# Hybrid attention and RWKV-7 decoder step: RWKV inputs through DRAM, one evicting engine per scan half-step, a rotating bank for odd scans, other queues for stores

## The chip, the cores and the metric

One core of a Trainium2 chip runs the whole program. The time is device microseconds of one execution, lower is better. The kernel before takes 2656.18 us, the median of three runs (2654.99, 2656.18, 2662.91).

The engines are named as the profile names them: PE (TensorE, matrix products; PEld is its weight load), DVE (VectorE), ACT (ScalarE), POOL (GpSimd), SP (the engine that here only issues DMAs). A "q" behind a name (SPq, ACTq, POOLq) means that engine's DMA issues.

## What is computed

One decoder layer, 2048 wide, for a prompt of 512 tokens and 8 single-token decode requests that share the weights. Everything is f32. The part around the change is the first sub-layer:

```python
h = _modulate(_rmsnorm(x, g_norm_mix[l]), sh1, sc1)        # adaLN: sh1 .. gt2 = silu(c) @ w_ada + b_ada
proj = h @ w_in[l]
q, k, v, p_rwkv = jnp.split(proj, ATTN_SPLITS, axis=-1)
...                                                        # sliding-window attention on q, k, v
rw, S, last_row = _rwkv7_mix(p_rwkv, shift0, S0, ...)
x = x + gt1[:, None, :] * (jnp.concatenate([att, rw], axis=-1) @ w_out[l])
...                                                        # then a SwiGLU feed-forward, then a final norm
```

RWKV-7 has 16 heads of 64. From the columns of `p_rwkv` (each mixed with the row of the token before) come r, k, v, a decay w, a gate, and vectors a and b. Per token and head a 64 x 64 state moves on:

```python
sa = jnp.einsum("bhij,bhj->bhi", S, a_t)
S = S * w_t[:, :, None, :] + sa[..., None] * b_t[:, :, None, :] + v_t[..., None] * k_t[:, :, None, :]
y = jnp.einsum("bhij,bhj->bhi", S, r_t)
```

The outputs are the two y, the new keys and values, the new RWKV states and the shift rows.

## The kernel before

**Main products.** Each f32 weight tile is split into a high part `wh` (a cast on ACT) and a low part `wl` (a subtraction on DVE), and the activations into H and L; a product is three fp32r matmuls, wh x H, wh x L and wl x H (`unit`, `mm3`, L98). `main_tile` makes one 128-column tile of `proj`: 16 k steps, each of 6 matmuls (128x128 weights, 260 columns: 256 tokens and 4 decode rows per half), with a new 128x512 weight tile every 4 k steps. `w_in` has 39 such column tiles: 5 are made in the startup (three tiles of low-rank inputs, and the first k and r tiles), 34 in the RWKV stage: 22 further RWKV inputs (k, r and v of 8 head pairs, less the two made early) and 12 for attention, which are "spilled" to DRAM (`filler`, tiles `sp`).

**Background work.** The RWKV work and the rest of the adaLN product run as Python generators beside the main tiles. After every k step `pump` adds 0.62 us to a reckoned PE clock and lets each generator whose own reckoned time has come emit its next piece. So the code writes its instructions in an interleaved order. A scheduler then orders them: each engine takes the earliest written instruction that its model holds ready, so the final order can differ from the written one where something is not ready yet.

**The RWKV chain of a head pair** (8 pairs, hp = 0 .. 7):
- `w_in_tile(8+hp)`, `(hp)`, `(16+hp)` make k, r and v. Each is evicted by ACT into a tile `pc`, of which there are four (the "ring"); a tile is held in PSUM, or spill tiles are put in ahead, until a ring place is free.
- `rwkv_prep1`: token shift (`shift_mix`, on POOL and DVE), the low-rank decay and rate products (PE tiles `pw`, `pa`, with weights `lf`), exponentials, norms and reciprocals, then transposes and small products per 32-token chunk (`pT`, `pG`). The chunk matrix `AB` goes to DRAM (`ABd`) and comes back spread over partitions (`As`) by four DMAs.
- `rwkv_prep2`: the same for r and v (`pA`, `pb`; tiles `RR`, `LS`, `BV`).
- `rwkv_rest`: a triangular solve of 31 steps on DVE (`stmp`, `Tt`), again a round trip through DRAM (`TTd`, `Td`), products `pu`, and then **the scan**: 16 chunks, each of two half-steps. Half-step A multiplies `L3` (128 rows by 32 columns, two heads) with the state tile `Z` into one PSUM tile `psc` and evicts 32x64 per head to Z: head 0 by DVE, head 1 by ACT. Half-step B multiplies `LS` (128 by 64) with Z into `psc` and evicts 64x64 per head, scaled by the chunk's decay `PC`: head 0 by DVE, head 1 by ACT. Each half-step needs the one before. Then come `pY`, a group norm, the gate (`pg`) and a store to `catd`.

Small products stand on PE between main products. The adaLN generator (`ada_gen`) adds one group of 4 matmuls (128x32 weights, tile `ada`, input tile `ar`) per k step; the `ar` tiles (three of them) also take what is spilled.

**Queues.** SP issues all weight loads, half of the `As` and `TTd` transfers, the spills and the stores to `catd`. POOL issues the other half.

**Behind the stage** come attention, the output projection (`po`), and the feed-forward (more than half of the time), none of which the diff edits.

Of the kernel before, what the change touches and what calls it, by code (L numbers as in the profile page):

```python
# [7 lines left out]
F32 = mybir.dt.float32  # L8
# [6 lines left out]
P = 128  # L15
# [13 lines left out]
I_WA, I_G0, I_G1 = 24, 25, 26  # L29

# [21 lines left out]

class PacedCore:
# [10 lines left out]
class Kern:  # L64
    def __init__(self, tc, I, O, upto="all"):
        self.tc, self.nc, self.I, self.O, self.upto = tc, tc.nc, I, O, upto
# [67 lines left out]
    def start(self, gen):  # L134
        self.bg.append([gen, 0.0])
# [13 lines left out]
    def run(self):  # L149
        tc, nc, I = self.tc, self.nc, self.I  # L150
        R = dict(side="right")
        with ExitStack() as st:
# [3 lines left out]
            self.load_consts()  # L156
            self.catd = [self.dr.tile([P, 512], F32, name=f"catd{i}") for i in range(16)]
# [10 lines left out]
            with ExitStack() as st2:  # L168
# [28 lines left out]
                self.drain()  # L197
                right.close()
# [105 lines left out]
    def ada_gen(self):  # L304
        nc = self.px
        for c in (GT1, SH2, SC2, GT2):
            for q in range(4):
                ci = c // 4 + q
                ps = self.hold("ada")
                for k in range(KD):  # L310
# [8 lines left out]
                    yield  # L319
                    yield  # L320
# [49 lines left out]
    def startup(self):  # L370
# [25 lines left out]
        self.pcs, self.ring, self.used = {}, [], set()  # L396
# [5 lines left out]
        self.start(self.seq(self.h_parts(xk, rstd), self.ada_gen()))  # L402
# [37 lines left out]
    def w_in_tile(self, idx):  # L440
        nc = self.nc
        src, m = self.w_in_src(idx)
        while len(self.ring) >= 4 and self.ring[-4] not in self.used and len(self.spills) > 2:
            self.filler()
        ps = self.main_tile(src, self.hH, self.hL, m)
        while len(self.ring) >= 4 and self.ring[-4] not in self.used:
            self.pump()
        pc = self.new_pc(idx)
        nc.scalar.copy(pc[:m, 1:513].rearrange("p (h t) -> p h t", h=2), ps[:m, :, 0:256])
        nc.scalar.copy(self.SC[:m, idx], ps[:m, :, 255:260])  # L450

    def filler(self):
# [8 lines left out]
        nc.scalar.copy(t.rearrange("p (h t) -> p h t", h=2), ps[:, :, 0:256])  # L461
        nc.vector.tensor_copy(scols, ps[:, :, 256:260])
        nc.sync.dma_start(dram, t)
# [11 lines left out]
    def rwkv_phase(self):  # L475
# [36 lines left out]
        nc.scalar.copy(self.SG1[64:128], self.SG1[0:64].bitcast(F32))  # L512
        pairs = [{"ready": True, "done": True, "chain": True, "prep1": True, "solved": True}] * 3
        for hp in range(8):
            d = {"hp": hp, "prev": pairs[-1], "prev2": pairs[-2], "prev3": pairs[-3]}
            pairs.append(d)
            for idx, job in ((8 + hp, self.seq(self.rwkv_prep1(d), self.rwkv_rest(d))), (hp, None),
                             (16 + hp, self.rwkv_prep2(d))):
                if idx not in self.pcs:
                    self.w_in_tile(idx)  # L520
                if job:
                    self.start(job)
# [14 lines left out]
    def recip(self, t, n=4):  # L537
        w = 512 // n
        for i in range(n):
            self.px.vector.reciprocal(t[:, i * w:(i + 1) * w], t[:, i * w:(i + 1) * w])  # L540
            yield

# [4 lines left out]
    def rwkv_prep1(self, d):  # L547
        nc, I, rp, rc = self.px, self.I, self.rp, self.rc
        hp = d["hp"]
        while not {"ready", "prep1"} <= d["prev"].keys() or "done" not in d["prev3"]:  # L550
            yield
# [7 lines left out]
        d["PC"] = PC = rc.tile([P, 16], F32, tag="PC", bufs=3, name=self.nm("PC"))  # L559
        lw = self.lora(hp, 0)  # L560
# [3 lines left out]
        for _ in range(3):  # L564
            yield
# [7 lines left out]
        nc.scalar.activation(A, pw, AF.Tanh, bias=self.w0h[:, hp:hp + 1], scale=0.5)  # L573
        ta = t512("tD")
# [19 lines left out]
        yield from self.recip(nrm)  # L594
# [8 lines left out]
        yield  # L603
# [6 lines left out]
        yield  # L610
# [7 lines left out]
        while "solved" not in d["prev"]:  # L618
            yield
# [14 lines left out]
        q2 = (self.nc.gpsimd, self.nc.sync)  # L634
# [1106 lines left out]
```

## Time and profile before

| | |
|---|---|
| profiled execution | 2657.76 us |
| its span, first to last instruction | 2656.0 us |
| median of three runs | 2656.18 us |
| startup, to the first decay product | 158 us |
| RWKV stage, with the 34 column tiles | 158 to 927 us |
| attention and output projection | 927 to 1209 us |
| feed-forward | 1209 to 2656 us |

How to read the rows. A group row (by line, or by tile) gives line, engine, operation, out<-in, the shapes (a PE row names rows*columns of the weights first), the count, then busy time and mean ns, and behind the last bar the engine's idle time ahead of these instructions, with what ended it. A tile row gives minimum, median and maximum duration in ns, and the first and last start in us. A wait row reads "engine line waited for: us in total, times, longest". A window row gives the stretch, its length, the busy time of PE, PEld, DVE, ACT and POOL with their instruction counts, the granted TensorE clock, the DMA share and GB/s. A timeline row gives start, time, instruction and count, and in brackets the idle time before it and what ended it. Calls through a helper that keeps reckoned times all carry the helper's line, L49. Matmuls are pipelined, so the times of neighbours overlap; the distance from start to start is what one costs.

### The profile page before, as it was taken

The page shows a single profiled execution, that of the slowest core. Times are in us where ns is not written, and L with a number is a line of the kernel's source. Part 1 is how long each engine was busy: PE and PEld are TensorE (multiplying, and loading weights), DVE is VectorE, ACT ScalarE, POOL GpSimd, SP SyncE. Part 2 cuts the span into 40 slices and gives each one's busy share as a digit, 9 for nine tenths or more (in the row PEclk, how much of TensorE's full clock was granted, in tenths as well). Part 3 has the DMA queues.
Part 4 walks back from the last instruction along what each step waited for, and adds up shares of the span by engine and source line. Part 5 has one row for each costly group of instructions (what it writes and reads, how often), then busy time and mean ns, then how long its engine had stood idle before and what let it go on. Part 6 is the DMA issues. An engine that isn't in the chain of part 4 may idle for free. (4 is left out here: it accounts for less than half of the span.)

```text
span 2656.0 us, 59166 instructions
## 1 busy us (share of the span) xinstructions
PE 2554.5 (96%) x23373; PEld 2340.7 (88%) x23373; DVE 1723.8 (65%) x3880; ACT 1105.9 (42%) x2153; POOL 382.5 (14%) x525
## 2 busy tenths in 40 slices
PE   7899999999999999998999999999999999999997
PEld 4677777888787889898999999999999999999997
DVE  5466767777657444678777777777777763444456
ACT  3133444545533324547544444444444532222225
POOL 0012112112112000021111212111121100000004
PEclk9999999999989999999999999999999999999999
DMA  9855445455546675245777777777777552333333
GB/s 347 294 165 154 152 126 162 149 166 160 159 153 207 203 251 146 94 160 183 191 201 204 193 208 198 191 207 198 194 208 200 155 184 92 124 125 102 116 105 106
DMA packets 241704, 460.22 MB, mean 173 GB/s; under 512 B 32353, under 2 KB 44561, under 8 KB 241393
## 3 DMA queue, kind: packets, MB, share of 16 engines
q1 hardware_dynamic: 206880, 379.88, 44.5%
q0 software_dynamic: 33904, 75.50, 13.4%
q8 instruction: 183, 3.00, 0.5%
q10 hardware_dynamic: 640, 1.05, 0.2%
q14 instruction: 97, 0.79, 0.1%
HBM read 421.73 MB, written 35.59 MB: 172 GB/s over the span
## 5 line engine op out<-in xcount | busy, mean ns | idle before, releaser
L88 ACT CAST wh<-raw 128x512 fp32r<-128x512 f32 (+2 forms) x410 | 246.9, 606 | 510.5 <-PE pf L98 278.9
L98 PE MATMUL pf<-go,wh 128*128 128x260 f32 x2560 | 414.1, 281 | 0.0
L91 DVE TENSOR_TENSOR wl<-raw,wh 128x512 fp32r<-128x512 f32 (+2 forms) x410 | 283.8, 694 | 200.4 <-ACT wh L88 194.8
L98 PEld LDWEIGHTS pf<-go,wh 128*128 128x128 f32 x2560 | 354.0, 188 | 0.1
L98 PE MATMUL pm<-hH,wh 128*128 128x260 f32 (+1 forms) x1248 | 301.3, 319 | 7.3 <-ACT wh L88 6.7
L1269 ACT CAST wh<-sr 128x512 fp32r<-128x512 f32 x320 | 198.1, 621 | 261.7 <-PE pm L1439 232.0
L1270 DVE TENSOR_TENSOR wl<-sr,wh 128x512 fp32r<-128x512 f32 x320 | 220.6, 690 | 83.0 <-ACT wh L1269 75.9
L98 PE MATMUL pm<-hH,wl 128*128 128x260 f32 (+1 forms) x1248 | 265.4, 292 | 5.2 <-DVE wl L91 5.1
L98 PE MATMUL pf<-go,wl 128*128 128x260 f32 x1280 | 267.7, 282 | 0.0
L1439 PE MATMUL pm<-xT,wh 128*128 128x260 f32 x1408 | 263.2, 286 | 4.4 <-DVE pc L1516 4.3
L98 PE MATMUL pm<-hL,wh 128*128 128x260 f32 (+1 forms) x1248 | 263.4, 291 | 0.0
L1439 PE MATMUL pm<-T,wh 128*128 128x260 f32 x1408 | 257.6, 283 | 0.0
L98 PEld LDWEIGHTS pm<-hH,wh 128*128 128x128 f32 (+1 forms) x1248 | 196.5, 191 | 57.8 <-issue 31.6
L1439 PEld LDWEIGHTS pm<-xT,wh 128*128 128x128 f32 x1408 | 216.9, 188 | 11.0 <-DVE pc L1516 6.1
L1439 PEld LDWEIGHTS pm<-T,wh 128*128 128x128 f32 x1408 | 216.9, 188 | 0.0
L98 PEld LDWEIGHTS pm<-hH,wl 128*128 128x128 f32 (+1 forms) x1248 | 197.4, 192 | 16.0 <-DVE wl L91 8.7
L1439 PE MATMUL pm<-B0H,wl 128*128 128x260 f32 x704 | 201.4, 286 | 9.6 <-DVE wl L1270 9.1
L98 PEld LDWEIGHTS pm<-hL,wh 128*128 128x128 f32 (+1 forms) x1248 | 196.9, 191 | 7.5 <-issue 5.2
L1439 PE MATMUL pm<-B0H,wh 128*128 128x260 f32 x704 | 200.3, 285 | 2.0 <-DVE acct L1206 1.7
L98 PEld LDWEIGHTS pf<-go,wl 128*128 128x128 f32 x1280 | 200.9, 188 | 0.0
L1439 PE MATMUL pm<-B0L,wh 128*128 128x260 f32 x704 | 198.9, 282 | 0.0
L1439 PE MATMUL pm<-T,wl 128*128 128x260 f32 x704 | 198.7, 282 | 0.0
(427 smaller groups left out, 5243.8 us busy)
## 6 DMA issues: line engine op xcount, KB each, us to landing
ar<-in_w_ada SPq DMA_DIRECT2D x256, 256.0 KB, 3.1
sr<-in_w_fi SPq DMA_DIRECT2D x176, 256.0 KB, 4.6
raw<-in_w_fo SPq DMA_DIRECT2D x176, 256.0 KB, 2.6
raw<-in_w_in SPq DMA_DIRECT2D x144, 256.0 KB, 3.7
araw<-in_w_ada SPq DMA_DIRECT2D x64, 512.0 KB, 6.5
raw<-in_w_fi SPq DMA_DIRECT2D x120, 256.0 KB, 4.6
s<-in_w_fi SPq DMA_DIRECT2D x80, 256.0 KB, 4.4
s<-in_w_fi POOLq DMA_DIRECT2D x80, 256.0 KB, 5.1
```

Of the source, the lines that this page charges most:

```text
L88: nc.scalar.copy(wh[:, :n], raw[:, :n])
L91: nc.vector.tensor_tensor(wl[:, :n], raw[:, :n], wh[:, :n].bitcast(F32), ALU.subtract)
L98: nc.tensor.matmul(ps[:m, bank, :HB], w, a[:, k, h, :], start=first and i == 0, stop=last and i == 2, skip_group_check=True,)
L1269: nc.scalar.copy(H, src)
L1270: nc.vector.tensor_tensor(L, src, H.bitcast(F32), ALU.subtract)
L1439: nc.tensor.matmul(ps[:, :HB], x[:, s], y, start=g == k == i == 0, stop=g == 1 and k == 3 and i == 2, skip_group_check=True)
```

## The change

- **Inputs through DRAM.** `w_in_tile` no longer waits for a ring place: it evicts to an `ar` tile, stores that to a new DRAM tile `pwd` from ACT's queue and goes on. A new generator `fetch_pc` loads the `pc` tiles from `pwd` on POOL's queue when the ring has a place. All 8 pairs' generators are started at once, then the 22 tiles are made in a row, then the 12 spills.
- **One evicting engine per half-step.** Half-step A: both heads by ACT. Half-step B: both heads by DVE. The extra 0.2 us that the generator reckoned per half-step is gone, and the two heads stand "side by side" as two evictions of one engine.
- **Odd scans in a rotating bank.** Even pairs keep the fixed tile `psc`; odd pairs take a new tile `pz` for each half-step from the two rotating PSUM tiles that all other small products use.
- **Queues.** The transfers of `As`, `TTd` and the store to `catd` are all issued by POOL; spill stores by ACT.
- **Yields and reckoned times.** The solver yields every second step, two reciprocals go in one piece, three empty yields go, reckoned times of 3 and 4 us stand behind DMAs, the low-rank weight tile `lf` has a lock, and the adaLN generator comes last in each `pump`.
- **Order left free.** Classes that could pin PE's order to the written one, and a counter that could pump more rarely, are added and set to off (`pinned` False, `every` 1).

```diff
     def pump(self, us=0.62):
         self.now(us)
-        for job in list(self.bg):
-            if job[1] > self.now():
+        self.calls += 1
+        if self.calls % self.every:
+            return
+        for job in sorted(self.bg, key=lambda job: job[2]):
+            if job[1] > self.now() + SLACK * (self.every - 1):
                 continue
...
     def w_in_tile(self, idx):
         nc = self.nc
-        src, m = self.w_in_src(idx)
-        while len(self.ring) >= 4 and self.ring[-4] not in self.used and len(self.spills) > 2:
-            self.filler()
-        ps = self.main_tile(src, self.hH, self.hL, m)
-        while len(self.ring) >= 4 and self.ring[-4] not in self.used:
-            self.pump()
-        pc = self.new_pc(idx)
-        nc.scalar.copy(pc[:m, 1:513].rearrange("p (h t) -> p h t", h=2), ps[:m, :, 0:256])
+        ps = self.main_tile(self.I["w_in"][idx], self.hH, self.hL)
+        t = self.w.tile([P, 512], F32, tag="ar", bufs=3, name=self.nm("sp"))
+        nc.scalar.copy(t.rearrange("p (h t) -> p h t", h=2), ps[:, :, 0:256])
+        nc.scalar.dma_start(self.pwd[idx], t)
...
+    def fetch_pc(self, order):
+        for idx in order:
+            while idx not in self.made or self.ring[-4:][0] not in self.used and len(self.ring) >= 4:
+                yield
+            pc = self.new_pc(idx)
+            del self.pcs[idx]
+            self.nc.gpsimd.dma_start(pc[:, 1:513], self.pwd[idx])
+            self.done_at = self.now() + 3.5
+            yield
+            self.pcs[idx] = pc
+            yield
...
+        self.start(self.fetch_pc(order))
         for hp in range(8):
...
+            self.start(self.seq(self.rwkv_prep1(d), self.rwkv_rest(d)))
+            self.start(self.rwkv_prep2(d))
+        for idx in order:
+            self.w_in_tile(idx)
...
-        q2 = (self.nc.gpsimd, self.nc.sync)
+        q2 = (self.nc.gpsimd, self.nc.gpsimd)
...
+        place = lambda: self.aux("pz") if hp % 2 else self.aux_c(0)
         for c in range(16):
-            ps = self.aux_c(hp % 2)
+            ps = place()
...
-            nc.vector.tensor_copy(Z[96:128, c, 0], ps[96:128, 0:64])
-            nc.scalar.copy(Z[96:128, c, 1], ps[64:96, 0:64])
-            self.done_at += 0.2
-            yield
+            for e, o in ((0, 96), (1, 64)):
+                nc.scalar.copy(Z[96:128, c, e], ps[o:o + 32, 0:64])
+            yield
+            ps = place()
...
             for e in range(2):
                 ro = slice(64 * e, 64 * e + 64)
-                if e:
-                    nc.scalar.activation(dst[:, e], ps[ro, 64:128], AF.Copy, scale=PC[ro, c:c + 1])
-                else:
-                    nc.vector.tensor_scalar(dst[:, e], ps[ro, 64:128], PC[ro, c:c + 1], None, ALU.mult)
-            self.done_at += 0.2
+                nc.vector.tensor_scalar(dst[:, e], ps[ro, 64:128], PC[ro, c:c + 1], None, ALU.mult)
             yield
...
-        nc.sync.dma_start(self.catd[hp], yc)
+        nc.gpsimd.dma_start(self.catd[hp], yc)
```

What this makes of the order shows in the first scan. PE, pair 0, before: a half-step A (psc from `L`, that is L3), twelve main products (pm, two k steps) and the adaLN group, then half-step B (psc from LS).

```order
L49 MATMUL psc<-Z_1732,L_283_1776 32x64 x2
L98 MATMUL pm_3127<-hH,wh_3334 128x260 x2
L98 MATMUL pm_3127<-hL,wh_3334 128x260 x2
L98 MATMUL pm_3127<-hH,wl_3335 128x260 x2
L98 MATMUL pm_3127<-hH,wh_3334 128x260 x2
L98 MATMUL pm_3127<-hL,wh_3334 128x260 x2
L98 MATMUL pm_3127<-hH,wl_3335 128x260 x2
L314 MATMUL ada_3202<-ar_3350,cT 32x128 x4
L49 MATMUL psc<-Z_1732,LS_1736 64x64 x2
```

Twelve main products (six rows of two) and the adaLN group lie between A and B, and B follows the adaLN group directly. PE, the same scan, in the changed kernel (every PE line is L64 there, since all calls pass through the new class):

```order
L64 MATMUL psc<-Z_1756,L_283_1800 32x64 x2
L64 MATMUL pm_3306<-hL,wh_3387 128x260 x2
L64 MATMUL pm_3306<-hH,wl_3388 128x260 x2
L64 MATMUL psc<-Z_1756,LS_1760 64x64 x2
L64 MATMUL ada_3351<-ar_3352,cT 32x128 x4
L64 MATMUL pm_3306<-hH,wh_3387 128x260 x2
L64 MATMUL pm_3306<-hL,wh_3387 128x260 x2
L64 MATMUL pm_3306<-hH,wl_3388 128x260
L64 MATMUL ada_3351<-ar_3407,cT 32x128
L64 MATMUL psc<-Z_1756,L_283_1800 32x64 x2
```

Between A and B stand 4 main products, between B and the next A 5 and parts of two adaLN groups; the groups are cut at any point. In the odd scan of pair 1, on PE in the changed kernel, the two heads' products of one half-step are also torn apart:

```order
L64 MATMUL pz_3997<-Z_1757,L_371_2372 32x64
L64 MATMUL pm_4409<-hL,wh_4504 128x260
L64 MATMUL pm_4409<-hH,wl_4505 128x260
L64 MATMUL pz_3997<-Z_1757,L_371_2372 32x64
L64 MATMUL pm_4409<-hH,wl_4505 128x260
L64 MATMUL ada_4206<-ar_4458,cT 32x128
L64 MATMUL pz_4014<-Z_1757,LS_1762 64x64 x2
```

Each half-step has a tile pz of its own there. On DVE, in the scan of pair 0 before, one head's scaled eviction is followed by seven solver instructions (stmp, Tt) of the next pair up to the next eviction:

```order
L49 TENSOR_SCALAR Z_1732<-psc,PC_1777 64x64
L49 TENSOR_TENSOR Tt<-Tt,stmp_3190 128x3x22
L49 TENSOR_TENSOR stmp_3213<-Tt,As 128x63
L49 TENSOR_TENSOR Tt<-Tt,stmp_3213 128x3x21
L49 TENSOR_TENSOR stmp_3238<-Tt,As 128x60
L49 TENSOR_TENSOR Tt<-Tt,stmp_3238 128x3x20
L49 TENSOR_TENSOR stmp_3274<-Tt,As 128x76
L49 TENSOR_TENSOR Tt<-Tt,stmp_3274 128x4x19
L49 COPY Z_1732<-psc 32x64
```

On DVE in the changed kernel, in the scan of pair 2, both heads' evictions are DVE's, with a solver instruction between them:

```order
L50 TENSOR_SCALAR Z_1756<-psc,PC_3375 64x64
L50 TENSOR_TENSOR stmp_4923<-Tt,As 128x28
L50 TENSOR_SCALAR Z_1756<-psc,PC_3375 64x64
L50 TENSOR_TENSOR Tt<-Tt,stmp_4923 128x28
L50 TENSOR_TENSOR stmp_4944<-Tt,As 128x54
L50 TENSOR_TENSOR Tt<-Tt,stmp_4944 128x2x27
L50 TENSOR_TENSOR stmp_4947<-Tt,As 128x52
L115 TENSOR_TENSOR wl_5975<-raw_5972,wh_5974 128x512
L50 TENSOR_TENSOR Tt<-Tt,stmp_4947 128x2x26
L50 TENSOR_SCALAR Z_1756<-psc,PC_3375 64x64
```

So DVE's evictions stand closer together than before, with less solver work ahead of each.

More of the change, by code (lines that the diff above doesn't have):

```diff
@@ L29 @@
 I_WA, I_G0, I_G1 = 24, 25, 26
+SLACK = 0.5
 class Paced:
@@ L50, in __getattr__, with __init__, call @@
         return call
+class InOrder:
+    def __init__(self, kern, eng):
+        self.kern, self.eng = kern, eng
+    def __getattr__(self, name):
+        f = getattr(self.eng, name)
+        def call(*a, **kw):
+            ins = f(*a, **kw)
+            return self.kern.tc.keep_in_program_order(ins) if self.kern.pinned else ins
+        return call
+class Core:
+    def __init__(self, kern, nc):
+        self.tensor = InOrder(kern, nc.tensor)
+        self.vector, self.scalar, self.gpsimd, self.sync = nc.vector, nc.scalar, nc.gpsimd, nc.sync
 class PacedCore:
@@ L65, in __init__ @@
     def __init__(self, tc, I, O, upto="all"):
-        self.tc, self.nc, self.I, self.O, self.upto = tc, tc.nc, I, O, upto
+        self.tc, self.I, self.O, self.upto = tc, I, O, upto
+        self.pinned, self.every, self.calls = False, 1, 0
+        self.nc = Core(self, tc.nc)
         self.n = 0
@@ L132, in pump, with start @@
             job[1] = self.done_at
-    def start(self, gen):
-        self.bg.append([gen, 0.0])
+    def start(self, gen, late=False):
+        self.bg.append([gen, 0.0, late])
     def drain(self):
@@ L156, in run @@
             self.load_consts()
+            self.pwd = [self.dr.tile([P, 512], F32, name=f"pwd{i}") for i in range(24)]
             self.catd = [self.dr.tile([P, 512], F32, name=f"catd{i}") for i in range(16)]
@@ L197, in run @@
                 self.drain()
+                self.pinned, self.every = False, 1
                 right.close()
@@ L395, in startup @@
         rstd = self.rstd_of(self.t520("tF"), ps)
-        self.pcs, self.ring, self.used = {}, [], set()
+        self.lf = False
+        self.pcs, self.ring, self.used, self.made = {}, [], set(), set()
         head = []
@@ L512, in rwkv_phase @@
         nc.scalar.copy(self.SG1[64:128], self.SG1[0:64].bitcast(F32))
+        self.pinned, self.every = False, 1
         pairs = [{"ready": True, "done": True, "chain": True, "prep1": True, "solved": True}] * 3
+        order = [i + hp for hp in range(8) for i in (8, 0, 16)]
+        order = [i for i in order if i not in self.pcs]
+        self.start(self.fetch_pc(order))
         for hp in range(8):
@@ L535, in aux_c, with recip, take_lf @@
         return self.psc[:, half]
[L537 to L540, printed above, removed]
+    def recip(self, t, per):
+        for i in range(4):
+            self.px.vector.reciprocal(t[:, i * 128:(i + 1) * 128], t[:, i * 128:(i + 1) * 128])
+            self.done_at += 0.5
+            if i % per == per - 1:
+                yield
+    def take_lf(self):
+        while self.lf:
             yield
+        self.lf = True
     def lora(self, hp, c0):
@@ L563, in rwkv_prep1 @@
         nc.scalar.activation(sq, k, AF.Square, scale=col(P_KK))
-        for _ in range(3):
-            yield
+        self.done_at = max(self.done_at, self.now() + 3)
+        yield
         pw = self.aux("pw")
```

48 lines of the change are left out of this document (24 added, 24 removed).

## The prediction

> **What bounds the kernel now.** I read the busy shares of the page first, then the engines by stage, then what TensorE (PE) waits for in the one stage whose instructions move, and last its timeline. The page, parts 1 and 2:
>
> ```profile
> PE 2554.5 (96%) x23373; PEld 2340.7 (88%) x23373; DVE 1723.8 (65%) x3880; ACT 1105.9 (42%) x2153; POOL 382.5 (14%) x525
> PE   7899999999999999998999999999999999999997
> ```
>
> PE is the bound everywhere, so only its path counts. The order of its instructions is the same in both kernels up to the first decay product (tile pw), and again from some 200 products behind the first output-projection product (tile po) on. These two rows of first and last starts (tiles pw and po) say where that is in time, and the windows say what the engines do between:
>
> ```profile
> L49 PE MATMUL pw<-LWA,lf x16: 393/501/503, 158.1 to 673.5; 128*128 128x512 f32 x16
> L98 PE MATMUL po<-cH,wh x512: 277/282/585, 926.7 to 1207.2; 128*128 128x260 f32 x171
> 158.00:927.00 769.00, 739.14 (x8263) 602.85 (x8256) 515.69 (x1337) 331.26 (x713) 138.29 (x193) 0.97 0.53 163
> 927.00:1209.00 282.00, 268.31 (x2299) 246.98 (x2297) 167.89 (x539) 128.66 (x322) 31.26 (x52) 0.97 0.49 158
> ```
>
> So the case is decided in 769 us, the RWKV stage: PE 739 us busy, VectorE (DVE) 516, ScalarE (ACT) 331. What PE waits for there is little (the waits of PE, then of ACT and of SP's DMA queue, in this window):
>
> ```profile
> PE psc L49 <- ACT Z L49: 14.0, 22, 1.6
> PE ada L314 <- DMA ar<-in_w_ada: 10.7, 11, 2.9
> PE pm L98 <- DVE wl L91: 1.6, 1, 1.6
> ACT Z L49 <- DVE Z L49: 197.2, 160, 4.3
> SPq L463 <- ACT sp L461: 23.2, 7, 10.2
> SPq L637 <- DMA ABd<-AB: 16.7, 7, 5.0
> ```
>
> All PE waits of the window add up to 28 us (three of 1.1 and less are not shown). That is all a better flow could give back. ACT's 197 us and SP's 40 us of waiting sit on engines that are not the bound.
>
> The rest of the stage is work, and part of it is the price of mixing small products into the large ones. The groups of the window by form:
>
> ```profile
> L98 PE MATMUL pm<-hH,wh 128*128 128x260 f32 x1086 | 264.2, 320 | 0.0
> L98 PE MATMUL pm<-hL,wh 128*128 128x260 f32 x1086 | 229.7, 291 | 0.0
> L98 PE MATMUL pm<-hH,wl 128*128 128x260 f32 x1088 | 229.5, 290 | 1.6 <-DVE wl L91 1.6
> ```
>
> These 3260 main products stand at one per 769/3260 = 0.236 us with everything between them. The timeline of PE in a stretch without waits shows their own pitch and what an interruption costs (columns: start, time, instruction, count):
>
> ```profile
> 301.39 0.40 PE L98 MATMUL pm<-hH,wl 128*128 128x260 f32 x2
> ...
> 301.72 0.42 PE L314 MATMUL ada<-ar,cT 128*32 128x128 f32 x8
> 302.08 0.34 PE L49 MATMUL psc<-Z,LS 128*64 128x64 f32 x4
> 302.35 0.51 PE L98 MATMUL pm<-hH,wh 128*128 128x260 f32 x2
> 302.69 0.40 PE L98 MATMUL pm<-hL,wh 128*128 128x260 f32 x2
> 302.93 0.40 PE L98 MATMUL pm<-hH,wl 128*128 128x260 f32 x2
> ...
> 303.98 0.43 PE L314 MATMUL ada<-ar,cT 128*32 128x128 f32 x8
> 304.24 0.28 PE L49 MATMUL psc<-Z,L 128*32 128x64 f32 x4
> 304.45 0.50 PE L98 MATMUL pm<-hH,wh 128*128 128x260 f32 x2
> 304.79 0.40 PE L98 MATMUL pm<-hL,wh 128*128 128x260 f32 x2
> ```
>
> A pair of main products takes 0.24 us (302.69 to 302.93), but 0.33 as the last pair ahead of a small group (301.39 to 301.72) and 0.34 as the first behind one (302.35 to 302.69). One interruption costs 0.09 + 0.10 = 0.19 us beyond the small group's own time.
>
> **Term 1, more interruptions.** In the order of before, PE leaves the main products 398 times in this stage, in that of the changed kernel 514 times: with no room between two scan steps, the steps no longer join an adaLN group (ada) at the end of a k step but fall between any two main products, and the two products of one step are torn apart 42 times. That is 116 more. Lower bound 0.10 us each (one end only), 12 us; upper 0.36, the whole distance from an ada group's start to the step behind it (301.72 to 302.08), 42 us. I take 0.22, near the row: **+25 us**.
>
> The Trainium skill (TensorEngine Tiling (Array Packing), Key Properties) says that changing the tiling mode, not just the tile, drains TensorE. The rows agree: after ada (128x32) the 128x32 step starts 0.26 later, the 128x64 step 0.36. Counted by that rule, the changes of mode go from 867 to 1085; at half of 0.19 each the term would be 218 x 0.095 = 21 us and the forecast 4 us lower.
>
> **Term 2, the scan.** Each of the 8 scans has 32 half-steps, A (psc from L3, evicted to Z) and B (psc from LS, scaled by PC). In the order of before, 10.0 main products stand on average between two half-steps; in the changed one 4.9 in 298 gaps (5.7 per half-step), and 3 or fewer in 135 gaps, of which 42 are only torn pairs. The scans fill 24.6 of the 34 main tiles now and 14.5 afterwards. At 0.236 us each, the room falls from 2.36 to 5.7 x 0.236 = 1.35 us. The chain needs the group on PE, a hop, two evictions and a hop. The rows (tile psc, then the timeline of DVE, ACT and PE):
>
> ```profile
> L49 DVE COPY Z<-psc x128: 229/230/231, 270.8 to 884.3; 32x64 f32<-32x64 f32 x128
> L49 ACT COPY Z<-psc x128: 203/203/206, 271.1 to 884.5; 32x64 f32<-32x64 f32 x128
> L49 DVE TENSOR_SCALAR Z<-psc,PC x120: 265/276/278, 272.9 to 882.8; 64x64 f32<-64x64 f32 x120
> L49 ACT ACTIVATE Z<-psc,PC x120: 311/311/313, 273.3 to 883.2; 64x64 f32<-64x64 f32 x120
> 293.89 0.95 DVE L49 RECIPROCAL tF<-tF 128x128 f32<-128x128 f32 x1
> 294.87 0.28 DVE L49 TENSOR_SCALAR Z<-psc,PC 64x64 f32<-64x64 f32 x1
> 295.18 0.31 ACT L49 ACTIVATE Z<-psc,PC 64x64 f32<-64x64 f32 x1 [1.83 <-DVE Z L49]
> 295.55 0.31 PE L49 MATMUL psc<-Z,L 128*32 128x64 f32 x4 [0.46 <-ACT Z L49]
> ```
>
> The two evictions run one after the other today (DVE ends at 295.15, ACT starts at 295.18). So one engine for both costs no overlap: A is 2 x 0.203 in place of 0.230 + 0.203, B 2 x 0.276 in place of 0.276 + 0.311. With the group at 0.31 and 0.34 and about 0.2 of hops between engines (0.03 and 0.06 of it in the last three rows), A needs 0.92 and B 1.10 us at the least. To that comes waiting behind other work on the evicting engine: half of a mean instruction (ACT 331/713 = 0.46, DVE 516/1337 = 0.39), some 0.2 us, and sometimes 0.95 (the reciprocal above). So A 1.1, B 1.3, against a mean room of 1.35: the mean just fits, the short gaps do not. Of the 93 whole gaps with at most 3 main products (0.36 us, and 0.2 for the interruption, and the group itself: about 0.8 in all), each waits about 0.4: 37 us, less the 14.0 that is there now: **+23 us**. Lower bound: all these waits vanish, -14. Upper: each of the 256 half-steps waits 0.35 us (1.35 of room against 1.7 with a 0.7 us instruction ahead each time), 90 - 14 = +76. I stay nearer the middle because the order was laid with the evictions in mind.
>
> **Term 3, queues and buffers.** Rows for the moved issues (tiles As, RR; landing times of the DMA list):
>
> ```profile
> L637 POOL DMA_DIRECT2D As<-ABd x16: 494/516/548, 197.5 to 712.6; - x16
> L49 ACTq DMA_DIRECT2D RR<-tC x8: 468/469/515, 191.8 to 723.8; - x8
> As<-ABd POOLq DMA_DIRECT2D x16, 128.0 KB, 3.6
> qd<-sp SPq DMA_DIRECT2D x8, 256.0 KB, 3.5
> ```
>
> ACT gets 34 store issues (22 inputs, 12 spills): 34 x 0.47 = 16 us, against 40 us of scaled evictions that it loses and 26 of copies that it gains: even, and hidden at 43% load. DVE gains 128 x 0.276 and loses 128 x 0.230: +6 us at 67%, hidden. POOL (18%) gets 22 fetches, 8 stores to catd and 4 issues per pair from SP (32): 62 x about 0.5 = 31 us, on no path while PE has main products to run, and up to 2 us per pair on the solver's round trip through DRAM. Traffic: 22 x 256 KB out and in, 11.5 MB in 769 us, 15 GB/s beside 163. SP loses issues and the waits of 23 and 17 us; PE waited 1.6 us for weights, so there is nothing to win there. Where it can hurt: each of the 22 inputs now takes one of three ar buffers for a store (3.5 us), and the adaLN products already wait 10.7 us for reloads of ar. Bounds -11 (those waits end) and 22 x 1 = +22; I take **+4 us**. The inputs' ring no longer holds w_in tiles back, but that hold did not leave PE idle, so freeing it is worth nothing. The pinned order and the rarer pumping are switched off everywhere (pinned False, every 1) and do nothing.
>
> **Sum.** The profiled execution took 2657.76 us (span 2656.0). 2657.8 + 25 + 23 + 4 = 2709.8; it lies 1.6 above the median shown, so **2708 us**. A measurement of this kernel can tell about 0.3% (8 us) from no change.
>
> **Rivals.**
> - *Slower by one-engine eviction.* If two engines could evict a pair side by side, giving both to one would lengthen A by 0.18 us (0.41 against 0.23) and B by 0.24 (0.55 against 0.31), 128 x 0.42 = 54 us, and 2762 in all. Against it: ACT started after DVE's end in the rows, and waited for it 160 times, so there is no overlap to lose. Chance 3%. The Trainium skill (the same page, PSUM Bottleneck) advises to evict with both ScalarE and VectorE; by it this rival would be likely, and this trace doesn't bear it out for two evictions of one bank.
> - *POOL's queue becomes the wait.* Fetches, round trips and the shift subtraction stand in one line; a fetch behind a TTd store waits for the solver. If each of 8 pairs comes 10 us late and PE, in order, stands at its first product: 2790. For it: today SP takes half of the solver's transfers. Against it: each input is fetched ahead, and pw stands a tile later than before. 8%.
> - *Even.* All 28 us of waits vanish and the interruptions cost their 25: 2653. 11%.
> - *Faster.* SP free of stores, ACT free of its 197 us behind DVE, so every adaLN load and eviction is early and PE never waits. Then 28 us go, and the kernel is faster as soon as an interruption costs under (28 - 8)/116 = 0.17 us; at 0.10 it is 2656 + 12 - 28 = 2640. For it: 0.10 is measured at either end. Against it: half the room between steps is gone. 10%.
>
> The forecast has 68%, with a range of its own from 2672 to 2768. Slower holds 0.79 (68 + 8 + 3), no change 0.11, faster 0.10. Leaving out the faster case below and part of the POOL case above: 2655 to 2768.
>
> **What would show it.** Term 1: pm from hH above 320 ns on average, more PE rows of the scan alone between main products. Term 2: psc waiting for Z well above 14 us, split over ACT (A) and DVE (B), PE's idle time rising in 158 to 927 and nowhere else. Term 3: ada waiting for ar above 10.7 us. po starting near 979 us instead of 926.7 carries the sum. Wrong if PE's waits in the stage fall under 28 us, or if POOL is named as what PE's chain waits for.

## The result, and the profile after

The changed kernel takes 2797.2 us (median of four runs, 2792.4 to 2813.4) against 2655.6 us for the kernel before (four runs, 2651.9 to 2662.9): a ratio of 1.054, 95% interval 1.049 to 1.059. It is slower by 142 us; 2708 was forecast, with 2768 as the upper end.

The profiled execution after took 2813.39 us (span 2811.6), the longest of the four and 155.6 more than the profiled one of before. The page, parts 1 and 2:

```profile
PE 2669.8 (95%) x23373; PEld 2404.8 (86%) x23373; DVE 1718.5 (61%) x3880; ACT 1087.1 (39%) x2151; POOL 414.1 (15%) x587
PE   7999999899899989999899999999999999999997
PEclk9998999869899899899999999999999999999999
```

PE's busy time grew by 115 us although its instruction count is the same, 23373. The row PEclk shows one reason: the granted clock of PE falls below 0.9 in six slices of the first half, to 0.6 in one; in the kernel before a single slice shows an 8. The first products of the output projection (tile po), and the windows up to them and of one stretch inside:

```profile
L64 PE MATMUL po<-cH,wh x512: 277/282/584, 1075.0 to 1360.1; 128*128 128x260 f32 x171
158.00:1075.00 917.00, 847.46 (x8285) 660.50 (x8284) 513.84 (x1341) 313.94 (x714) 170.03 (x256) 0.91 0.48 149
542.00:604.00 62.00, 62.00 (x424) 44.66 (x421) 20.53 (x67) 8.65 (x31) 4.88 (x9) 0.50 0.33 98
```

po starts at 1075.0 in place of 926.7, so 148 of the 156 us arise in the RWKV stage, as the prediction said; most of the rest goes with another stretch of lowered clock in the attention part (half clock from 1174 to 1198 us). In the stage PE idles 917.0 - 847.5 = 69.5 us (before 29.9). And its clock is 0.91 on average, 0.50 through the whole of 542 to 604, where PE never pauses. The trace's clock records know only full and half; in the stage they add up to 157 us at half (before 41). PE's waits in the stage:

```profile
PE ada L64 <- DMA ar<-in_w_ada: 34.0, 35, 3.4
PE pu L64 <- DVE TT L50: 7.0, 5, 2.7
PE pt L64 <- DVE RR L50: 5.1, 4, 2.8
PE pT L64 <- DVE tA L50: 2.7, 2, 1.4
PE pz L64 <- ACT Z L50: 2.5, 4, 1.2
```

The scan hardly waits: pz 2.5, and psc 0.7 in the group rows, against 14.0 before. adaLN's wait for ar has gone from 10.7 to 34.0. The group rows of the main products (mean ns behind the busy time):

```profile
L64 PE MATMUL pm<-hH,wh 128*128 128x260 f32 x1092 | 271.5, 319 | 1.7 <-ACT wh L112 1.3 <-DVE SC L469 0.3
L64 PE MATMUL pm<-hL,wh 128*128 128x260 f32 x1092 | 255.6, 306 | 0.0
L64 PE MATMUL pm<-hH,wl 128*128 128x260 f32 x1092 | 255.3, 307 | 1.9 <-DVE wl L115 1.9
```

The last two rise from 290 to 306 ns, the first stays at 319 (320 before), so this sign of Term 1 did not show. The timeline of PE inside the stretch at half clock, in an odd scan:

```profile
556.25 0.48 PE L64 MATMUL pz<-Z,LS 128*64 128x64 f32 x4
556.66 0.66 PE L64 MATMUL ada<-ar,cT 128*32 128x128 f32 x8
557.25 0.80 PE L64 MATMUL pm<-hH,wh 128*128 128x260 f32 x2
557.98 0.42 PE L64 MATMUL pz<-Z,L 128*32 128x64 f32 x2
558.33 0.80 PE L64 MATMUL pm<-hL,wh 128*128 128x260 f32 x2
559.06 0.42 PE L64 MATMUL pz<-Z,L 128*32 128x64 f32 x2
559.41 0.80 PE L64 MATMUL pm<-hH,wl 128*128 128x260 f32 x2
```

A pair of main products from a small group to the next takes 0.73 us (557.25 to 557.98) where the even pitch before, inside a run of them, was 0.24, and each is followed by a torn half of a scan step. No row has an idle bracket: PE itself is the bound, at half speed, with an interruption every two products.

### The profile page after: what moved, and what is told of

It is laid out like the page before. It is cut to its first block, busy times and chain, and to the rows that moved or that the text cites. A ratio compares the mean times of both kernels' runs of the same rounds, so it can differ in the third digit from the quotient of the medians.

```text
span 2811.6 us, 59209 instructions
## 1 busy us (share of the span) xinstructions
PE 2669.8 (95%) x23373; PEld 2404.8 (86%) x23373; DVE 1718.5 (61%) x3880; ACT 1087.1 (39%) x2151; POOL 414.1 (15%) x587
## 5 line engine op out<-in xcount | busy, mean ns | idle before, releaser
L64 PE MATMUL pf<-go,wh 128*128 128x260 f32 x2560 | 414.1, 281 | 0.0
L64 PEld LDWEIGHTS pf<-go,wh 128*128 128x128 f32 x2560 | 353.9, 188 | 0.1
L64 PE MATMUL pm<-hH,wh 128*128 128x260 f32 (+1 forms) x1248 | 308.3, 319 | 8.5 <-ACT wh L112 7.8
L64 PE MATMUL pm<-hH,wl 128*128 128x260 f32 (+1 forms) x1248 | 291.3, 308 | 5.0 <-DVE wl L115 5.0
L64 PE MATMUL pm<-hL,wh 128*128 128x260 f32 (+1 forms) x1248 | 289.1, 305 | 0.0
L64 PE MATMUL pm<-xT,wh 128*128 128x260 f32 x1408 | 263.0, 286 | 8.2 <-DVE pc L1566 8.1
L64 PE MATMUL pf<-go,wl 128*128 128x260 f32 x1280 | 267.7, 282 | 0.0
L64 PE MATMUL pm<-T,wh 128*128 128x260 f32 x1408 | 257.7, 283 | 0.0
L64 PEld LDWEIGHTS pm<-hH,wh 128*128 128x128 f32 (+1 forms) x1248 | 206.4, 197 | 59.2 <-issue 39.4
L64 PEld LDWEIGHTS pm<-hH,wl 128*128 128x128 f32 (+1 forms) x1248 | 206.6, 198 | 31.7 <-issue 14.9
L64 PEld LDWEIGHTS pm<-xT,wh 128*128 128x128 f32 x1408 | 216.7, 188 | 14.8 <-DVE pc L1566 9.9
L64 PEld LDWEIGHTS pm<-hL,wh 128*128 128x128 f32 (+1 forms) x1248 | 206.5, 197 | 21.4 <-issue 14.8
L64 PEld LDWEIGHTS pm<-T,wh 128*128 128x128 f32 x1408 | 216.9, 188 | 0.0
L64 PE MATMUL pm<-B0H,wl 128*128 128x260 f32 x704 | 200.9, 286 | 8.6 <-DVE wl L1320 8.3
L64 PE MATMUL pm<-B0H,wh 128*128 128x260 f32 x704 | 200.0, 284 | 2.4 <-ACT wh L1319 1.5
L64 PEld LDWEIGHTS pf<-go,wl 128*128 128x128 f32 x1280 | 201.0, 188 | 0.0
L64 PE MATMUL pm<-B0L,wh 128*128 128x260 f32 x704 | 198.9, 283 | 0.0
L64 PE MATMUL pm<-T,wl 128*128 128x260 f32 x704 | 198.7, 282 | 0.0
```

The lines of the kernel that those rows point to most:

```text
L64: ins = f(*a, **kw)
```

## The experiments

All ratios are to the kernel before, run on the same chip, with 95% intervals. Four theories name the suspects: **F** the free order, **D** the inputs through DRAM, **E** the one evicting engine or the bank, and **G** (from the second group on) that dense interruptions hold the granted clock down.

**The order held as written.** The first rival was the scheduler.

```diff
-        self.pinned, self.every = False, 1
+        self.pinned, self.every = True, 1
```

> The changed kernel with PE's order in the RWKV stage held to the written one (pinned True, every 1); everything else as changed, the DRAM inputs, the one evicting engine, the rotating bank and the queues with it. Counted in the order, PE leaves the main products 421 times (514 unpinned, 398 before) and 4 gaps between scan steps hold 3 or fewer main products (135 unpinned). Theory F (the free order is the cause: steps, adaLN groups and the products pu and pt laid where they are not ready on the chip, PE waits there, and the clock dips behind such places): PE's waits in the stage fall from some 68 to 30 us or less, the half-clock stretches of the stage from some 157 to 60 us or less, and the time falls to 2650 to 2700 us. Theory D (the inputs through DRAM share the three ar buffers with the adaLN loads): adaLN's waits for ar stay at 30 us or more and the time at 2750 or more. Theory E (one evicting engine or the rotating bank): psc and pz waiting for Z become the main wait, time above 2730.

2816.0 us, 1.059 (1.055 to 1.063): no better. The changes of mode fell back to 850, but PE idled 141 us:

```profile
PE pu L64 <- DVE TT L50: 37.3, 6, 10.1
PE ada L64 <- DMA ar<-in_w_ada: 30.1, 20, 4.9
PE psc L64 <- DVE Z L50: 14.7, 11, 3.6
```

F fell: the free order trades waits for interruptions at about the same price.

**Parts alone, on the kernel before.** Inputs through DRAM (the new `w_in_tile` and `fetch_pc`, all pairs started at once):

> The kernel before with only the inputs through DRAM: stores from ACT's queue into an ar tile's DRAM copy, fetches by POOL, all pairs started at once; scans, banks and the other queues as before. The order hardly changes: PE leaves the main products 421 times (398 before), mean gap between scan steps 10.1 (10.0). Theory D: adaLN's waits for ar rise from 10.7 to 30 us or more, and the time to 2700 or more. Theory F and E: 2650 to 2680, adaLN's waits below 20 us.

2695.9 us, 1.012 (1.010 to 1.015). adaLN waits 19.1 us for ar, less than D asked, and the time lies between the two forecasts. One evicting engine per half-step, without the reckoned 0.2 us:

> The kernel before with only the scan's evictions changed: half-step A by ACT alone, half-step B by DVE alone, and without the 0.2 us reckoned per half-step. PE leaves the main products 434 times (398 before), mean gap between steps 7.4 (10.0), 31 gaps of 3 or fewer main products (4). Theory E: psc waits for Z rise from 14 to 40 us or more, the time to 2700 or more. Theory F: 36 more interruptions at 0.2 us and somewhat shorter gaps cost some 5 to 25 us: 2660 to 2685. Theory D: as before, 2650 to 2670.

2677.1 us, 1.005 (1.004 to 1.007); psc waits only 5.3 us for Z. Next, PE's order held and the background emitted at every second k step in the changed kernel (`pinned, every = True, 2`):

> The changed kernel with both switches on: PE's order held to the written one and the background emitted at every second k step (pinned True, every 2). PE leaves the main products 226 times, changes of mode 687 (before 398 and 867), mean gap between steps 10.8 products, 32 gaps of 3 or fewer. Theory F with 0.2 us per interruption: 172 fewer than before, 34 us less than the order held at every k step, 2615 to 2660, if PE's waits stay below 40 us. Theory D: no gain, above 2720, with adaLN waiting for ar. Theory E: steps with two groups in a row wait for the evictions, above 2680.

2753.7 us, 1.034 (1.030 to 1.038): fewer changes of mode, and 89 us more idle time. adaLN waits 49.6 us for ar there, as D forecast.

**The clock by itself.** The half-clock stretches called for a measurement without the layer.

```python
for n, wait in PLAN:                 # n = 24, 12, 8, 6, 5, 4, 3, 2 with a wait, 6, 4, 3, 2 without
    self.main(w, 250)                # pure main products
    if wait:
        w = self.gap(wait)           # new weights at the end of a DVE chain: PE waits 4.4 us
    for _ in range(reps):            # about 60 us
        self.main(w, n)
        self.small()                 # two small products, 128x32 and 128x64 weights in turn
```

> A kernel of its own, without the layer: blocks of n main products (128x128 weights, 260 columns) followed by one scan-like pair of small products (128x32 or 128x64 weights, 64 columns, no eviction and no wait), n = 24, 12, 8, 6, 5, 4, 3, 2, each block about 60 us long, behind 250 pure main products and a wait of PE of about 4 us; then n = 6, 4, 3, 2 again without the wait. It shows what an interruption costs (time of a repeat less n x 0.12 us) and what density of interruptions does to the granted clock. Theory G (density holds the clock down: after a wait the clock halves, and comes back only where main products stand dense enough): half clock for one or two windows of 3.4 us for n of 12 and more, for the whole block for n of 6 or less; without the wait the same n stay at full clock, or fall only at n of 3 or less. Theory H (only waits lower the clock, and it comes back by itself): 3.4 to 7 us of half clock in every block, whatever n. Interruption: 0.19 us by the step of the prediction, 0.34 by the 13.4 us that the one-engine eviction cost for 36 more interruptions.

The trace's clock records give the half-clock time behind the wait as 6.8, 6.8, 10.2 and 6.8 us for n = 24, 12, 8 and 6; 34.1 us for n = 5; and for n = 4, 3 and 2 it lasts through the whole block into the pure products, 105.8, 102.4 and 102.4 us. Without a wait ahead, the blocks of 6, 4, 3 and 2 stand in one stretch of 389 us at full clock. The wait ahead of n = 12, then the windows of n = 12, 5 and 4 behind a wait, and of n = 4 without:

```profile
140.53 0.80 PE L39 MATMUL pm<-h,w 128*128 128x260 f32 x2 [4.41 <-DVE w L66]
144.00:202.00 58.00, 58.00 (x488) 51.53 (x489) 0.00 (x0) 0.00 (x0) 0.00 (x0) 0.99 0.00 1
430.00:502.00 72.00, 72.00 (x507) 56.84 (x506) 0.00 (x0) 0.00 (x0) 0.00 (x0) 0.77 0.00 1
538.00:636.00 98.00, 98.00 (x510) 74.29 (x508) 0.00 (x0) 0.00 (x0) 0.00 (x0) 0.50 0.00 1
1024.00:1082.00 58.00, 58.00 (x504) 44.31 (x503) 0.00 (x0) 0.00 (x0) 0.00 (x0) 1.00 0.00 1
```

The last two windows hold the same instructions, both with PE busy without a pause, and take 98 and 58 us. Their timelines, at half and at full clock (a pair of small f32 products has four records):

```profile
564.91 1.23 PE L39 MATMUL pm<-h,w 128*128 128x260 f32 x4
566.08 0.48 PE L39 MATMUL pz<-raw 128*64 128x64 f32 x4
566.49 1.24 PE L39 MATMUL pm<-h,w 128*128 128x260 f32 x4
...
1040.20 0.74 PE L39 MATMUL pm<-h,w 128*128 128x260 f32 x4
1040.88 0.31 PE L39 MATMUL pz<-raw 128*32 128x64 f32 x4
1041.11 0.75 PE L39 MATMUL pm<-h,w 128*128 128x260 f32 x4
```

One repeat takes 1.58 us (564.91 to 566.49) against 0.91 (1040.20 to 1041.11). For these blocks G holds, with the border at 5 products in place of 6, and H has fallen: a wait starts the half clock, density decides whether it ends. That a dense block starts no half clock by itself is shown only down to n = 2, which is about 10 main products in 3.41 us (an estimate: 2 x 3.41 / 0.69, the repeat being 0.24 + 0.45 us). The layer has thinner stretches; what they do stands under the missing term below. At full clock a repeat costs 0.44 to 0.45 us beyond n x 0.12, for two changes of mode and the small products, so one change costs at most 0.22.

**A wait that starts it, taken away.** adaLN's products read a constant tile; the loads go on, their use is left out.

```diff
-   self.cT[:, k, :], raw[:, j * 128:(j + 1) * 128],
+   self.cT[:, k, :], self.ident,
```

> The changed kernel with the adaLN products of the stage reading a constant tile in place of the loaded ar tile; the loads are still issued, so the traffic stays. It leaves out the use of the loaded weights, and with it only the wait for them (34 us in the changed kernel). PE leaves the main products 508 times (514). Theory G: the waits of 34 us go and with them about half of the starts of half-clock stretches; half clock in the stage falls from 157 to 60 to 110 us, time 2710 to 2745. If the dense scan lowers the clock without any wait: half clock stays near 157, time about 2760. Theory D (ar sharing is the main cause): 2690 or less.

2773.9 us, 1.040 (1.037 to 1.043): of the 5.4% only 1.4 came back, a miss for G's sizes and the end of D as the main cause. PE still idles 67 us and runs 137 us at half, which is nearest to the forecast in which the dense scan lowers the clock without any wait. Waits moved to the next late things:

```profile
PE pu L64 <- DVE TT L50: 21.4, 7, 6.5
PE ada L64 <- ACT adar L50: 5.7, 2, 5.0
```

**Two more parts alone, on the kernel before.** The bank for odd scans:

> The kernel before with only the odd scans in the rotating bank. PE leaves the main products 429 times (398), mean gap between steps 8.4 products (10.0), 49 gaps of 3 or fewer (4). At 0.19 to 0.34 us per interruption +6 to +11 us; if the steps wait for a place in the two rotating tiles, PE's waits rise by more than 10 us. 2660 to 2685.

2699.2 us, 1.013 (1.011 to 1.016). PE idles only 2.5 us more, but runs 92 us at half clock (41), with 82 more changes of mode; the time is above the 2685 of the forecast, which had no clock in it. The queues (`As`, `TTd`, `catd` all from POOL, spills from ACT):

> The kernel before with only the queues changed: the transfers of As and TTd and the stores to catd all from POOL, the spill stores from ACT. The order stays (390 interruptions against 398). If POOL's queue makes the solver's round trips late: PE waits for pu and pG, time above 2670. If the queues are hidden: 2645 to 2665, same as before.

2671.0 us, 1.003 (1.001 to 1.004): nearly nothing. POOL's queue is not the cause.

**Undoing, and what is left.** The scan of before in the changed kernel, the inputs of before in the changed kernel, and the kernel before with only the small edits (yields, reckoned times, lock, place of adaLN; also in them, and not in the list of the change above, the wait for the previous pair's solver moves from ahead of the products pG to ahead of the As loads, and the gate's low-rank weights are loaded earlier):

> The changed kernel with the scan as before: both engines evict each half-step, 0.2 us reckoned, fixed bank in every pair. Inputs through DRAM, queues, yields and reckoned times stay changed. TensorE's changes of mode in the order: 957 (changed 1085, before 867). The account read from the runs so far, time difference = difference of PE's idle time + half of the difference of half-clock time + 0.23 us per change of mode, gives 90 x 0.23 = 21 us for the modes. Theory G (dense steps keep the clock down): with mean gaps of 7.2 products in place of 4.9, half clock falls from 157 to 100 us or less, time 2700 to 2735. If the scan's part is only its own (one engine +13 and bank +35, alone): 2797 less 48, about 2750.

> The changed kernel with the inputs as before, from PSUM straight into the ring; everything else as changed. Changes of mode 1086 (1085). If the inputs through DRAM cost what they cost alone (+33 us): 2764, adaLN's waits for ar fall from 34 to 15 us or less. If the waits only move (as they did when adaLN read a constant tile): 2775 to 2800.

> The kernel before with only what the prediction put at nothing: fewer yields in solver, reciprocals and gate, reckoned times of 3 and 4 us behind DMAs, the lock on lf, the late place of the adaLN generator in each pump; inputs, scans and queues as before. Changes of mode 1017 (before 867), mean gap between steps 7.1 products (10.0). By the account 150 x 0.23 = 34 us, and more if PE waits: 2690 to 2720. If these edits are really nothing: 2650 to 2670.

2760.8 (1.037, 1.034 to 1.040), 2759.8 (1.038, 1.034 to 1.043) and 2730.5 us (1.025, 1.022 to 1.027). The scan undone lies above its forecast of 2700 to 2735 (half clock fell to 123 us only), the small edits above theirs of 2690 to 2720. Each undoing gives back about what the part cost alone, and the small edits, which had no term of their own in the prediction, are the largest part. The parts alone add up to 0.5 + 1.2 + 1.3 + 0.3 + 2.5 = 5.8%, against 5.4 (4.9 to 5.9) for all together. That they add up does not show that they act alone: one line of the small edits costs more than all of them, as the next runs show.

**Which small edit.** One alone on the kernel before, and its undoing (with that of the reciprocals) in the changed one:

```diff
             eng.tensor_tensor(Tt[:, 0:m, s + 1:32], Tt[:, 0:m, s + 1:32], tv, ALU.add)
-            yield
+            if s % 2:
+                yield
```

> The kernel before with one edit of the part that the prediction put at nothing: the solver yields at every second step. In the reckoned times the solver's DVE work then no longer holds the scan's steps apart: mean gap between steps 6.8 main products (10.0), 49 gaps of 3 or fewer (4), changes of mode 982 (867), interruptions 449 (398). Theory: this edit is the reason that all small edits together cost 65 us. By the account 115 x 0.23 = 26 us for the modes, and half clock and waits as in that kernel (22 + 12): 2700 to 2730. Rival: the reckoned times and the late adaLN generator are the reason, then 2665 to 2690.

> The changed kernel with only the solver yielding at every step again and each reciprocal a piece of its own. Changes of mode 1024 (1085), mean gap between steps 6.7 (4.9), 70 gaps of 3 or fewer (135). By the account 61 x 0.23 = 14 us for the modes; if half clock falls with the density of the scan to some 100 us, 28 us more: 2745 to 2770. If the density does not matter: 2780 to 2797.

2755.2 us, 1.032 (1.029 to 1.035), and 2736.8 us, 1.026 (1.024 to 1.027). This one line costs 3.2% alone, more than forecast, and its undoing with the reciprocals brings the changed kernel from 1.054 to 1.026. The window and PE's waits with this line alone:

```profile
158.00:1017.30 859.30, 801.09 (x8279) 634.38 (x8278) 501.06 (x1341) 330.90 (x714) 136.17 (x193) 0.94 0.49 146
```

```profile
PE ada L314 <- DMA ar<-in_w_ada: 17.9, 18, 2.3
PE pu L49 <- DVE TT L49: 13.0, 7, 3.8
PE psc L49 <- ACT Z L49: 9.9, 18, 1.6
```

It shows all three ills at once: 58 us of idle time (29.9 before), adaLN and the solver's result TT late, and a clock of 0.94 (0.97).

**Candidates for a faster kernel.** Pumping at every second k step in the kernel before; the small edits with the order held and every second k step; adaLN groups two at a time:

> The kernel before with the background emitted only at every second k step in the RWKV stage, the order left free; adaLN keeps its rate by fewer yields. Changes of mode 749 (before 867), interruptions 300 (398). By the account 118 x 0.23 = 27 us less if PE's idle time and the half-clock time stay: 2630 to 2645, faster than both kernels. If the emitted clumps are late on the chip as in the changed kernel with both switches on (89 us of idle time more): 2680 to 2740.

> A candidate: the kernel with only the small edits (inputs, scans and queues as before), with PE's order held to the written one and the background emitted at every second k step. Changes of mode 673 (before 867), interruptions 226 (398), mean gap between steps 11.8. By the account 194 x 0.23 = 45 us less; PE's waits rise if the clumps are late, as in the changed kernel with both switches (89 us), whose inputs went through DRAM. With 30 to 60 us more idle time and 20 us of half clock: 2640 to 2690; faster than before only below 40 us of added waits.

> A candidate: the kernel before with adaLN's groups emitted two at a time at every fourth yield, and of the small edits only the removed yields, the lock and the late adaLN generator (solver, reciprocals and reckoned times as before). Changes of mode 788 (867), mean gap between steps 10.7 (10.0), 9 gaps of 3 or fewer. By the account 79 x 0.23 = 18 us less if waits and half clock stay: 2640 to 2655. If two adaLN groups at once wait for their two loads (ada waiting for ar above 30 us): 2670 to 2700.

2721.0 (1.021, 1.019 to 1.023), 2743.7 (1.028, 1.025 to 1.030) and 2678.9 us (1.006, 1.003 to 1.009). None beats the kernel before. The first came out at the slower of its two forecasts and is instructive (windows to the last main product of the stage, and from there to po):

```profile
158.00:843.80 685.80, 665.13 (x7690) 558.32 (x7689) 434.17 (x1149) 286.97 (x605) 107.98 (x173) 0.99 0.57 168
843.80:989.60 145.80, 74.00 (x623) 52.98 (x621) 80.88 (x200) 36.70 (x101) 35.83 (x35) 0.57 0.45 145
```

Its main products end 83 us earlier than before, at a clock of 0.99, but the RWKV chain, emitted half as often, is not done, and its rest runs for 146 us without cover at 0.57. In the second, clumped steps really wait for their evictions:

```profile
PE psc L64 <- ACT Z L50: 64.6, 69, 2.6
```

**The account.** For every kernel, the later start of po against the sum of three differences to the kernel before: PE's idle time in the stage (window length less PE busy), half of its half-clock time (clock records), and 0.23 us per change of weight shape in PE's order (128x128 to 128x32 and so on). The 0.23 is fitted to the first eight rows; the last eight came later. The half is taken, not measured: by the blocks above half clock costs 1 - 0.926/1.55 = 0.40 of its time, and with 0.40 the best price per change would be 0.25 and the first eight rows would agree only within 15 us.

| kernel | po later, us | idle | half clock / 2 | changes x 0.23 | sum |
|---|---|---|---|---|---|
| changed | 148.3 | 39.7 | 58.0 | 218: 50.1 | 147.8 |
| order held | 144.0 | 111.1 | 44.3 | -17: -3.9 | 151.5 |
| DRAM inputs alone | 43.9 | 23.9 | 13.6 | 41: 9.4 | 47.0 |
| one engine alone | 13.4 | 3.0 | -1.8 | 55: 12.6 | 13.9 |
| held, every 2 | 96.3 | 89.4 | 46.0 | -180: -41.4 | 94.0 |
| ada constant | 117.7 | 37.2 | 47.8 | 152: 35.0 | 120.0 |
| bank alone | 50.1 | 2.5 | 25.6 | 82: 18.9 | 47.0 |
| queues alone | 3.5 | -2.9 | 3.4 | 2: 0.5 | 1.0 |
| scan undone | 98.2 | 24.0 | 41.0 | 90: 20.7 | 85.6 |
| DRAM undone | 97.9 | 23.8 | 22.2 | 219: 50.4 | 96.4 |
| small edits alone | 70.1 | 11.6 | 22.2 | 150: 34.5 | 68.2 |
| every 2 on before | 62.9 | 62.6 | 47.2 | -118: -27.1 | 82.7 |
| solver yield alone | 90.6 | 28.3 | 30.7 | 115: 26.5 | 85.5 |
| solver undone | 75.1 | 12.2 | 22.2 | 157: 36.1 | 70.5 |
| small edits, held, every 2 | 87.4 | 89.8 | 27.3 | -194: -44.6 | 72.5 |
| ada in twos | 15.1 | 12.1 | 7.3 | -79: -18.2 | 1.2 |

The first eight agree within 8 us, the later ones within 20, five of the eight within 13. With interruptions (runs of main products that PE leaves) in place of changes, at their own best price of 0.32 us, the 16 rows miss by 12 us in the mean (root mean square), with changes by 8. The account is a fit of sizes, not a proof of each term by itself. The largest miss (every 2 on before) has half-clock time in which PE idles too, which the sum counts twice.

## Why the prediction was right or wrong

**Place and sign: right.** The stage alone carries the loss; feed-forward takes the same (1447 and 1450 us), and PE stayed the bound. po came at 1075, not 979. The range up to 2768, with its 68%, ends 29 us short of the measured time.

**Term 1, more interruptions: right mechanism, half the size.** +25 us were put down; the account gives 50. The step that failed is the unit and its price: 116 interruptions at 0.22, or, as the prediction also reckoned, 218 changes of mode at half of an interruption's 0.19. When a step leaves its adaLN group, or its two products part, the number of changes is what rises, by 218, and each costs about 0.23 (at most 0.22 in the blocks, small products included, so the 50 is an upper figure), not 0.095. The rule of the Trainium skill (TensorEngine Tiling (Array Packing), Key Properties) that a change of mode drains the engine names the better count, and the account bears the count out, as changes fit the 16 rows better than interruptions do; the price had been taken too low.

**Term 2, the scan: wrong as told.** Waits of +23 us were forecast; psc and pz together wait 3.2 us for ACT's Z in place of 14.0. Steps 1.35 us apart on average do find their evictions done. The rival on one-engine eviction was rightly held small (13 us alone, most of it changes of mode). The wait exists only where steps are clumped (64.6 us above).

**Term 3, queues and buffers: too low.** +4 us, at most 22, were given; PE's idle time rose by 39.7. adaLN's wait rose by 23, at the upper end, but the buffers explain only part: with the inputs undone it is still 26.8 us, and with the wait taken away the idle time stays at 67. What is late is the whole chain of small steps, packed more tightly; remove one wait and the next shows. The rival on POOL's queue fell (6 us for the queues alone).

**The missing term: the granted clock, 58 us.** The sum had no row for it, though the window quoted 0.97. This is the largest failed step. In the stages of all 17 runs of the layer, from 158 us to the first po, lie 4168 whole windows of 3.41 us, the step of the clock records. Full clock was followed by half 120 times out of 127 where PE was busy under half of the window, and 63 times out of 3499 where it was busy 60% or more. From half, it stayed half 176 times out of 223 with fewer than 6 main products begun in the window, and 0 out of 59 with 12 or more. So a wait costs itself, and then up to 60 us of half speed if a dense scan follows. Ahead of the stretch from 542 stands one wait of 1.66 us:

```profile
540.50 0.34 PE L64 MATMUL pz<-Z,LS 128*64 128x64 f32 x4 [1.66 <-DVE L L50]
```

But a wait is not needed. Of all 204 falls from full to half, 44 come behind a window in which PE never idled (busy 99% or more), 5 of the 13 in the changed kernel, and 44 of its 157 us at half begin so. Out of such windows the clock fell 29 times in 49 with fewer than 4 main products, 15 in 228 with 4 to 9, and never in 2291 with 10 or more. One of these falls in the changed kernel, the windows and PE's timeline:

```profile
778.00:781.40 3.40, 3.40 (x56) 3.02 (x55) 1.69 (x4) 0.00 (x0) 0.00 (x0) 0.99 0.39 112
781.40:788.20 6.80, 6.80 (x94) 5.37 (x93) 3.13 (x11) 0.00 (x0) 0.75 (x2) 0.50 0.30 87
776.89 2.05 PE L64 MATMUL pA<-tC,KB 64*64 64x32 f32 x32
778.87 0.43 PE L64 MATMUL ada<-ar,cT 128*32 128x128 f32 x8
779.23 0.39 PE L64 MATMUL pm<-hH,wl 128*128 128x260 f32 x1
779.46 0.28 PE L64 MATMUL pm<-hH,wh 128*128 128x260 f32 x1
779.67 2.24 PE L64 MATMUL pA<-tC,KB 64*64 64x32 f32 x32
```

Two groups of small products (pA) stand round two main products, no row has an idle bracket, and the clock halves at 781.4. So the half clock is the price of density as well as of waits, which fits how little came back when one wait was taken away. What the chip counts is not shown; the number of main products in a window is only what tells the cases apart here. No run changes the density alone, so how the 58 us split between the two stays open.

The Trainium skill (TensorE: Matmul & The Clock Gate, Part 1: The HAM clock gate) tells of a window of 3413 ns behind which the clock falls or rises; the lengths here are its multiples. Its rule that one busy window releases the clock does not hold here, if busy is read by the profile's rows: PE was 100% busy from 542 to 604 and through the block of n = 4, and stayed at half.

**The order was counted, its cause was not looked for.** That the mean gap falls from 10.0 to 4.9 was put down to the dropped 0.2 us and the one engine. Alone these give 7.4, the solver's yield alone 6.8. In the order of before 70 half-steps have exactly 12 main products between them (two k steps) and 27 have 1 to 5; with the solver yielding at every second step these are 7 and 89. The solver's pieces, one per pump, had kept the reckoned DVE busy and so held the scan apart. That reading of the generator is argued from the code and the counts; the cost of the edit is measured. Why its 3.2% alone exceeds the 2.5% of all small edits together stays open: the changes of mode do not tell (982 and 1017), only the idle time and the half clock do.

## What to carry to other kernels

Count what interrupts a stream of large products by changes of weight shape, and look at the granted clock per stage before costing a tighter interleaving: a short wait followed by dense small products can run at half speed long after the wait is over, and a stretch of almost only small products can start it without a wait. A yield in a background generator is part of the schedule, so cost each such edit alone. When one wait is taken away and the time stays, look at what is late next.

## What the hardware showed that was not expected

The clock has a memory. The same instructions, n = 4 main products between small pairs with PE never idle, ran in 58 us (504 of them) when they came from full clock and in 98 us (510) when they came from half, and 5 or 6 products between the pairs are the border behind a wait (34.1 and 6.8 us of half clock). A PE that is always busy doesn't keep the clock up: in the layer it fell behind 29 of 49 fully busy windows with fewer than 4 main products. Half clock does not double the time: a repeat went from 0.926 to 1.55 us as a mean over the block, a factor of 1.67.
